# Filter time tiles of a long convolution taken in pairs: products in a tile of two PSUM banks

## The chip, the cores and the metric

The kernel runs on one core of a Trainium2 chip. The engines named below are TensorE (PE in the profile, its weight loads PEld), VectorE (DVE), ScalarE (ACT), GpSimd (POOL) and SyncE (SP), whose queue issues nearly all DMAs of this kernel. PSUM is the memory that TensorE writes; here it has eight banks of 512 fp32 columns on 128 partitions. The metric is the device time of one execution in microseconds; lower is better.

## The reference, cut to what matters

The model is two layers over 1024 latent and 256 context tokens of width 1024. Layer 0 is an attention layer, layer 1 a Hyena layer: two gated long convolutions. The filters of these convolutions aren't weights. A small network with sines makes them from position features, and an exponential decay in time is laid over them:

```python
def hyena_filter_spectra(L, w_in, w_hid, b, freq, w_out):
    ...
    for k, w in enumerate((w_in, w_hid[0], w_hid[1])):
        hdn = jnp.sin(freq[k] * (hdn @ w.astype(f32) + b[k]))
    h = (hdn @ w_out.astype(f32)).reshape(L, HY_ORDER, 2, HY_WIDTH)
    ...
    h = h * jnp.exp(-t * deltas)[:, None, None, :]
    hf, hb = h[:, :, 0], h[:, :, 1]
    k_circ = jnp.concatenate([hf[:1] + hb[:1], hf[1:], jnp.zeros_like(hf[:1]), hb[:0:-1]], axis=0)
    return jnp.fft.rfft(k_circ, axis=0)
```

There are 1024 time steps, two orders, two directions (forward and backward) and 1024 channels. The change concerns the line with the decay and the joining of the two directions.

## The kernel before, in words

**What runs beside what.** `layer0_in` opens the PSUM pool `ps0` with eight banks: three for projections (`pj`), one for the modulation vectors (`ad`), two for the filter products (tag `ph`) and two for the spectra (`pu`). It runs two generators against each other. `filters` makes the filter spectra of layer 1, which need nothing but constants. `work` makes the modulation vectors (`ada`, whose weights `adaw` are streamed through two pages) and the input projections of layer 0 (`project`: 12 matmuls of 512 columns for each step, with weights `wr` that are split into a high and a low part, L96 and L97). After each second step of `filters` comes one step of `work`. At the very start the steps of `filters` alternate with the eight steps of the first `ada`, four loads of 256 KB each.

**The filter loop.** `filter_mlp` (L181) computes the hidden activations of the network: three layers, each in two halves of 512 columns, matmul (L202), ScalarE (L203), VectorE and ScalarE again. Then 8 channel groups `g` of 128 channels follow, and in each group 8 time tiles `j` of 128 steps:

- L314 loads the decay table of the tile, 128 KB, into one of two buffers `dec`;
- four matmuls of 256 columns (L318, L319: two directions, high and low part of the weights `fw`) fill one bank, tile `ph`; two such tiles exist, so TensorE can fill one while VectorE reads the other;
- L321 multiplies the 512 columns by the decay, into `kk` (two buffers); in tile 0 a bias of one row is added (L325);
- L328 and L329 store the sum and the difference of the two directions, 256 columns each, into `kp` and `km`.

After the eight tiles, `load(g + 1)` splits the group's next weights `fwr` (an own buffer), and `ring` (L217) and `forward` (L267) take `kp` and `km` through a hand-made transform of eight blocks: some 20 VectorE operations, then for each block a split (L96, L97), 9 to 12 matmuls into `u`, a ScalarE eviction `ko` (L340) and two stores to `kd` in HBM (L351). `ring` takes two buffers of tag `rt` for three temporaries.

**What sets the order.** Each engine works off its own queue in order, and so does the SP queue: a DMA that waits for a buffer holds all that were issued behind it. The order within a queue is fixed when the program is built, from the order of the code and an estimate of when each thing is ready, so that the loads and the products of the next tiles can stand somewhat ahead of their place in the code. The attention follows when both generators are through and the pools are closed; its tiles take the space of the filter pools.

Of the kernel before, what the change touches and what calls it, by code (L numbers as in the profile page):

```python
# [11 lines left out]
F32 = mybir.dt.float32  # L12
F32R = mybir.dt.float32r
AF = mybir.ActivationFunctionType
ALU = mybir.AluOpType
# [4 lines left out]
P = 128  # L20
# [35 lines left out]
class Net:  # L56
# [124 lines left out]
    def filter_mlp(self, fp, mp, psum, ptag):  # L181
        nc, a = self.nc, self.a
        feat = mp.tile([66, L], F32, tag="rg", name="feat")
        nc.sync.dma_start(out=feat, in_=a["feat"])
        win = fp.tile([66, P], F32, name="fwin")
        whid = fp.tile([P, 2, P], F32, name="fwhid")
        nc.sync.dma_start(out=win, in_=a["fwin"])
        nc.sync.dma_start(out=whid, in_=a["fwhid"].rearrange("l p m -> p l m"))
        v, act = nc.vector, nc.scalar
        turn = fp.tile([P, 2, 3], F32, name="turn")  # L190
        v.tensor_scalar(out=turn[:, 0], in0=self.col("ff", 0, 3), scalar1=1 / (2 * math.pi), scalar2=None, op0=ALU.mult)
        v.tensor_tensor(out=turn[:, 1], in0=self.col("fb", 0, 3), in1=turn[:, 0], op=ALU.mult)
        h = feat
        magic = 12582912.0
        for l in range(3):
            w = win if l == 0 else whid[:, l - 1, :]
            arg = mp.tile([P, L], F32, tag="rg", name="arg")
            n = mp.tile([P, L], F32, tag="rg", name="nrnd")
            for s in range(2):
                sl = slice(512 * s, 512 * s + 512)  # L200
                ps = psum.tile([P, 512], F32, tag=ptag, name="pmlp")
                nc.tensor.matmul(ps, lhsT=w, rhs=h[:, sl], start=True, stop=True)  # L202
                act.activation(out=arg[:, sl], in_=ps, func=AF.Identity, scale=turn[:, 0, l : l + 1],  # L203
                               bias=turn[:, 1, l : l + 1])
                v.tensor_scalar(out=n[:, sl], in0=arg[:, sl], scalar1=magic, scalar2=-magic, op0=ALU.add, op1=ALU.add)
                v.tensor_tensor(out=arg[:, sl], in0=arg[:, sl], in1=n[:, sl], op=ALU.subtract)
                act.activation(out=n[:, sl], in_=arg[:, sl], func=AF.Sin, scale=TURN)
            h = n
        self.show("h", h)
        self.hf = fp.tile([P, L], F32R, name="hf")  # L210
        self.hr = fp.tile([P, L], F32R, name="hr")
        nc.scalar.copy(out=self.hf[0:64], in_=h[0:64])
        nc.vector.tensor_tensor(out=self.hf[64:128], in0=h[0:64], in1=self.hf[0:64], op=ALU.subtract)
        nc.scalar.copy(out=self.hr[64:128], in_=h[64:128])
        nc.vector.tensor_tensor(out=self.hr[0:64], in0=h[64:128], in1=self.hr[64:128], op=ALU.subtract)
# [68 lines left out]
    def filters(self, psum, pt_h, pt_u, side):  # L284
        nc, a = self.nc, self.a
        fp = self.open("filt", 1, side=side)
        rp = self.open("filtr", 2, side=side)
        gp = self.open("filtg", 6, side=side)
        fm = [fp.tile([P, 25, P], F32R, name=f"fm{i}") for i in range(2)]
        self.filter_mlp(fp, gp, psum, pt_h)  # L290
        last = yield
        for c in (slice(13, 19), slice(19, 25), slice(0, 7), slice(7, 13)):
            for i in range(2):
                nc.gpsimd.tensor_copy(out=fm[i][0:1, c.start, 0:1], in_=last[0:1, 0:1])
                nc.gpsimd.dma_start(out=fm[i][:, c], in_=a["fm"][i][:, c])
        two = lambda tag, dt=F32: rp.tile([P, 2, CS], dt, tag=tag, name=tag)
        ubank = lambda: psum.tile([P, 2, CS], F32, tag=pt_u, name="u")
        self.kd = self.dram.tile([2, NCH, P, 17, CS], F32, name="kd")

        def load(g):  # L300
            wr = rp.tile([P, 512], F32, tag="fwr", name="fwr", bufs=1)
            wh, wl = [rp.tile([P, 512], F32R, tag=f"fw{r}", name="fw", bufs=1) for r in range(2)]
            nc.sync.dma_start(out=wr, in_=a["fwout"][g])
            self.split(wr, wh, wl)
            return wh, wl

        nxt = load(0)
        for g in range(KD):
            wh, wl = nxt
            kp = [gp.tile([P, 4, CS], F32, tag="rg", name=f"kp{i}") for i in range(2)]  # L310
            km = [gp.tile([P, 4, CS], F32, tag="rg", name=f"km{i}") for i in range(2)]
            for j in range(8):
                dec = rp.tile([P, 2, 1, P], F32, tag="dec", name="dec", bufs=2)
                nc.sync.dma_start(out=dec, in_=a["dec"][g, j])  # L314
                ps = psum.tile([P, 2, 2, P], F32, tag=pt_h, name="ph")
                ts = slice(P * j, P * j + P)
                for d, h in ((0, self.hf), (1, self.hr)):
                    nc.tensor.matmul(ps[:, d], lhsT=h[:, ts], rhs=wh[:, 256 * d : 256 * d + 256], start=True, stop=False)  # L318
                    nc.tensor.matmul(ps[:, d], lhsT=h[:, ts], rhs=wl[:, 256 * d : 256 * d + 256], start=False, stop=True)  # L319
                kk = rp.tile([P, 2, 2, P], F32, tag="kk", name="kk")  # L320
                nc.vector.tensor_tensor(out=kk, in0=ps, in1=dec.broadcast_to([P, 2, 2, P]), op=ALU.mult)  # L321
                if j == 0:
                    bias = rp.tile([1, 2, P], F32, tag="hb", name="hbias", bufs=1)
                    nc.sync.dma_start(out=bias, in_=a["hbias"][:, :, P * g : P * g + P])
                    nc.vector.tensor_tensor(out=kk[0:1, 0], in0=kk[0:1, 0], in1=bias, op=ALU.add)  # L325
                k0 = kp[j // 4][:, j % 4].rearrange("p (o c) -> p o c", o=2)
                k1 = km[j // 4][:, j % 4].rearrange("p (o c) -> p o c", o=2)
                nc.vector.tensor_tensor(out=k0, in0=kk[:, 0], in1=kk[:, 1], op=ALU.add)  # L328
                nc.vector.tensor_tensor(out=k1, in0=kk[:, 0], in1=kk[:, 1], op=ALU.subtract)  # L329
                if j == 0:  # L330
                    nc.vector.tensor_copy(out=km[0][0:1, 0], in_=kp[0][0:1, 0])
                yield
            if g + 1 < KD:
                nxt = load(g + 1)
            cl = slice((g % 2) * P, (g % 2) * P + P)

            def emit(i, b):
                u = self.forward(two, ubank, fm, i, b)
                ko = rp.tile([P, 2, CS], F32, tag="ko", name="ko")
                nc.scalar.activation(out=ko, in_=u, func=AF.Copy, scale=1.0 / 1024)  # L340
                r0 = 2 * i + 1
                if i == 0:
                    r0 = 0
                    kx = rp.tile([P, CS], F32, tag="kx", name="kx", bufs=1)
                    nc.vector.tensor_scalar(out=ko[0:1], in0=ko[0:1], scalar1=0.5, scalar2=None, op0=ALU.mult)
                    nc.scalar.copy(out=kx, in_=ko[:, 0])
                    nc.scalar.copy(out=kx[0:1], in_=ko[0:1, 1])
                    nc.vector.memset(ko[0:1, 1], 0.0)
                for o in range(2):
                    oc = slice(P * o, P * o + P)  # L350
                    nc.sync.dma_start(out=self.kd[o, g // 2, :, r0 : r0 + 2, cl], in_=ko[:, :, oc])  # L351
                    if i == 0:
                        nc.sync.dma_start(out=self.kd[o, g // 2, :, 2, cl], in_=kx[:, oc])

            for i, b in self.ring(two, lambda: gp.tile([P, 1024], F32, tag="rg", name="rg"), kp, km, False):
                emit(i, b)
                yield
        self.close("filtg", "filtr", "filt")
# [989 lines left out]
def _features():  # L1348
    f = np.float32
    i = np.arange(L, dtype=f)  # L1350
    t = np.linspace(0.0, 1.0, L).astype(f)
    wpos = (f(2.0 * math.pi / L) * i)
    bands = np.linspace(1e-4, 15, 16).astype(f)
    ph = bands[None, :] * wpos[:, None]
    hdn = np.concatenate([t[:, None], np.cos(ph), -np.sin(ph)], axis=-1).astype(f)
    rev = (L - np.arange(L)) % L
    feat = np.concatenate([hdn.T, hdn[rev].T], axis=0)
    deltas = np.abs(np.linspace(math.log(1e-2) / 0.3, math.log(1e-2) / 1.5, D)).astype(f)
    dec = np.exp(-t[:, None] * deltas[None, :]).astype(f)
    dec = np.stack([dec, dec[rev]], axis=1)  # L1360
    dec = dec.reshape(8, P, 2, 8, P).transpose(3, 0, 1, 2, 4)
    return np.ascontiguousarray(feat), np.ascontiguousarray(dec[:, :, :, :, None, :])


def _rope():
# [9 lines left out]
def prepare(i):  # L1375
# [35 lines left out]
    a["fm"] = _dft(False)  # L1411
    a["dm"] = _dft(True)
    a["feat"], a["dec"] = _features()
    w = i["hy_filt_w_in"][0]
    o = np.zeros_like(w)
# [32 lines left out]
```

## Time and profile before

| | us |
|---|---|
| median of 3 runs | 1736.26 |
| lowest, highest | 1733.69, 1740.81 |
| profiled execution, its own time | 1731.71 |
| span of the profiled execution | 1729.9 |
| busy: TensorE, VectorE, ScalarE | 1633.5, 1442.2, 766.3 |

The filters and the input projections take the first quarter of the span, about 420 us. Shares of busy time over the whole span say little about that quarter: TensorE's 94% is mostly the attention and the convolutions behind it. So the views that count are those that can be cut to a stretch: the windows (busy time by engine in each stretch, the DMA share, bytes per second), the waits (who waited for whom), the chain of waits in order of time, and the timeline. Busy times of TensorE overstate it, because the records of neighbouring matmuls overlap; start to start, the matmuls of 512 columns stand 0.23 us apart, with durations of 0.39.

### The profile page before, as it was taken

To read this page: it belongs to the slowest core of one execution; us is meant where nothing else is said; L and a number is where in the kernel's file an instruction comes from. 1 tells how busy PE (TensorE), PEld (TensorE's weight loads), DVE (VectorE), ACT (ScalarE), POOL (GpSimd) and SP (SyncE) were. 2 spreads that over 40 slices of the span, in tenths; PEclk is the share of its full clock that TensorE was granted. 3 is DMA by queue.
4 is the path that set the end of the run, shared out by engine and by line. 5 is a ranking of instruction groups with operands and counts; after the bars stand their busy time and mean duration, and the time that the engine had idled before them with its cause. 6 is when DMAs were issued, how large, how long until landed. Compare 5 with 4: busy or idle time off the path is not lost.

```text
span 1729.9 us, 22940 instructions
## 1 busy us (share of the span) xinstructions
PE 1633.5 (94%) x8160; PEld 1299.5 (75%) x8160; DVE 1442.2 (83%) x2558; ACT 766.3 (44%) x1337; POOL 16.0 (1%) x43
## 2 busy tenths in 40 slices
PE   5899897899999999999999999999999999999996
PEld 2467676787788788788787777888888888887874
DVE  4886979895699899899899456999999999999856
ACT  4533444445455465555555345433433433343313
POOL 1000000000000000000000010000000000000000
PEclk9899999899999999999999999999999999999998
DMA  9777664436101001010014771332332332244545
GB/s 342 256 231 222 200 187 120 138 89 206 28 27 37 25 32 38 19 33 25 25 56 132 232 254 64 101 98 83 101 115 83 104 106 89 95 122 134 180 142 197
DMA packets 140759, 206.15 MB, mean 119 GB/s; under 512 B 13578, under 2 KB 71649, under 8 KB 140516
## 3 DMA queue, kind: packets, MB, share of 16 engines
q1 hardware_dynamic: 137508, 194.00, 35.7%
q0 software_dynamic: 3136, 10.69, 1.9%
q8 instruction: 64, 1.05, 0.3%
q14 instruction: 51, 0.42, 0.1%
HBM read 148.92 MB, written 53.61 MB: 117 GB/s over the span
## 4 chain that ended last, share of the span: by engine, by line
PE 75%; DVE 10%; DMA 9%; ACT 3%; issue 2%; SPq 1%; DVEq 0%; ACTq 0%
PE pj L121 12%; PE pj L119 12%; PE pj L120 12%; DMA dec<-in_dec 2%; PE O L120 2%; PE S L119 2%; PE O L119 2%; PE S L826 2%; PE O L121 2%; PE apx L762 2%; PE S L825 2%; PE S L121 2%; PE S L120 2%; PE apx L763 2%; PE fu L119 2%; PE fy L119 2%
## 5 line engine op out<-in xcount | busy, mean ns | idle before, releaser
L96 ACT CAST w<-wr 128x512 fp32r<-128x512 f32 (+1 forms) x149 | 90.7, 609 | 259.5 <-PE pj L120 129.5
L119 PE MATMUL pj<-a,w 128*128 128x512 f32 x512 | 203.1, 397 | 1.7 <-ACT a L422 1.6
L121 PE MATMUL pj<-a,w 128*128 128x512 f32 x512 | 203.1, 398 | 0.0
L120 PE MATMUL pj<-a,w 128*128 128x512 f32 x512 | 203.0, 397 | 0.0
L828 ACT ACTIVATE p<-S 128x512 f32<-128x512 f32 x160 | 95.7, 598 | 148.2 <-DVE acc L835 69.5
L97 DVE TENSOR_TENSOR w<-wr,w 128x512 fp32r<-128x512 f32 (+1 forms) x149 | 98.8, 671 | 54.7 <-ACT w L96 54.6
L96 ACT CAST bh<-raw 128x512 fp32r<-128x512 f32 x128 | 77.1, 620 | 89.1 <-DVE raw L1071 71.0
L119 PEld LDWEIGHTS pj<-a,w 128*128 128x128 f32 x512 | 96.4, 188 | 22.0 <-ACT a L422 2.4
L120 PEld LDWEIGHTS pj<-a,w 128*128 128x128 f32 x512 | 96.5, 188 | 19.9 <-DVE a L423 0.2
L121 PEld LDWEIGHTS pj<-a,w 128*128 128x128 f32 x512 | 96.6, 189 | 19.5 <-issue 0.8
L97 DVE TENSOR_TENSOR p<-p 128x512 fp32r<-128x512 f32 x160 | 109.4, 684 | 1.5 <-ACT p L96 1.2
L764 DVE TENSOR_REDUCE cm<-apx 128x1 f32<-128x512 f32 (+1 forms) x192 | 107.1, 591 | 3.8 <-PE apx L763 3.1
L835 DVE TENSOR_TENSOR acc<-acc,p 128x512 f32<-128x512 f32 x144 | 98.7, 685 | 7.6 <-ACT p L828 6.7
L121 PE MATMUL pj<-pg,w 128*128 128x512 f32 (+1 forms) x248 | 96.5, 389 | 8.7 <-DVE w L97 8.6
L96 ACT CAST p<-p 128x512 fp32r<-128x512 f32 x160 | 99.5, 622 | 4.8
L119 PE MATMUL pj<-pg,w 128*128 128x512 f32 (+1 forms) x248 | 95.7, 389 | 2.7 <-ACT pg L422 2.7
L120 PE MATMUL pj<-pg,w 128*128 128x512 f32 (+1 forms) x248 | 96.6, 389 | 0.6 <-DVE pg L423 0.6
L97 DVE TENSOR_TENSOR bl<-raw,bh 128x512 fp32r<-128x512 f32 x128 | 84.7, 686 | 9.1 <-ACT bh L96 9.0
L119 PE MATMUL u<-bh,fm 128*128 128x256 f32 (+1 forms) x200 | 68.2, 342 | 12.2 <-ACT bh L96 9.5
L762 PE MATMUL apx<-kn,qn 128*128 128x512 f32 (+1 forms) x192 | 69.0, 364 | 2.2 <-DVE cm L764 1.9
L321 DVE TENSOR_TENSOR kk<-ph,dec 128x512 f32<-128x512 f32 x64 | 42.6, 684 | 33.2 <-DMA dec<-in_dec 26.6
L763 PE MATMUL apx<-krh,r 128*128 128x512 f32 (+1 forms) x192 | 67.1, 357 | 0.0
(312 smaller groups left out, 4408.9 us busy)
## 6 DMA issues: line engine op xcount, KB each, us to landing
aw<-in_adaw SPq DMA_DIRECT2D x32, 512.0 KB
kd<-ko SPq DMA_DIRECT2D x128, 128.0 KB
wr<-in_hw SPq DMA_DIRECT2D x64, 256.0 KB
kt<-kd SPq DMA_DIRECT2D x56, 256.0 KB
wr<-in_w SPq DMA_DIRECT2D x34, 256.0 KB
dec<-in_dec SPq DMA_DIRECT2D x64, 128.0 KB
pg<-in_adaw SPq DMA_DIRECT2D x32, 256.0 KB
wr<-in_wo SPq DMA_DIRECT2D x32, 256.0 KB
```

What stands on the lines that cost most here:

```text
L96: self.nc.scalar.copy(out=hi, in_=raw)
L97: self.nc.vector.tensor_tensor(out=lo, in0=raw, in1=hi, op=ALU.subtract)
L119: mm(out, lhsT=w[0], rhs=x[0], start=start, stop=False)
L120: mm(out, lhsT=w[0], rhs=x[1], start=False, stop=False)
L121: self.last = mm(out, lhsT=w[1], rhs=x[0], start=False, stop=stop)
L321: nc.vector.tensor_tensor(out=kk, in0=ps, in1=dec.broadcast_to([P, 2, 2, P]), op=ALU.mult)
L762: mm(b[:, :w], lhsT=qn[0][:, c], rhs=kn[0][:, o : o + w], start=True, stop=False)
L763: mm(b[:, :w], lhsT=r1[:, c], rhs=krh[:, o : o + w], start=False, stop=True)
L764: v.tensor_reduce(out=cm[:, t, i : i + 1], in_=b[:, :w], axis=AX.X, op=ALU.max)
L825: mm(S, lhsT=krh[:, c], rhs=r1, start=False, stop=False)
L828: act.activation(out=p, in_=S, func=AF.Exp, scale=ASCALE)
L835: v.tensor_tensor(out=acc, in0=acc, in1=p, op=ALU.add)
```

## The change

Two time tiles are taken together. The products of a pair go into one PSUM tile of two banks, of which there is one (`bufs=1`). One decay product covers 1024 columns, sum and difference cover 512 each, one decay load brings 256 KB; `dec` still has two buffers, now of a pair each, and `kk` has one of a pair. The pair yields twice at its end, so the count of steps stays. The network's small matmuls (L202) use the same PSUM tag and so have one tile instead of two. The raw weights `wr` in `load` take a buffer of tag `rt` instead of their own. The decay tables are laid out anew on the host.

```diff
-                ps = psum.tile([P, 512], F32, tag=ptag, name="pmlp")
+                ps = psum.tile([P, 2, 512], F32, tag=ptag, name="pmlp", bufs=1)[:, s]
...
-            wr = rp.tile([P, 512], F32, tag="fwr", name="fwr", bufs=1)
+            wr = two("rt").rearrange("p a c -> p (a c)")
...
-            for j in range(8):
-                dec = rp.tile([P, 2, 1, P], F32, tag="dec", name="dec", bufs=2)
-                nc.sync.dma_start(out=dec, in_=a["dec"][g, j])
-                ps = psum.tile([P, 2, 2, P], F32, tag=pt_h, name="ph")
-                ts = slice(P * j, P * j + P)
-                for d, h in ((0, self.hf), (1, self.hr)):
-                    nc.tensor.matmul(ps[:, d], lhsT=h[:, ts], rhs=wh[:, 256 * d : 256 * d + 256], start=True, stop=False)
-                    nc.tensor.matmul(ps[:, d], lhsT=h[:, ts], rhs=wl[:, 256 * d : 256 * d + 256], start=False, stop=True)
-                kk = rp.tile([P, 2, 2, P], F32, tag="kk", name="kk")
-                nc.vector.tensor_tensor(out=kk, in0=ps, in1=dec.broadcast_to([P, 2, 2, P]), op=ALU.mult)
+            for j in range(0, 8, 2):
+                dec = rp.tile([P, 2, 2, 1, P], F32, tag="dec", name="dec", bufs=2)
+                nc.sync.dma_start(out=dec, in_=a["dec"][g, j // 2])
+                ps = psum.tile([P, 2, 2, 2, P], F32, tag=pt_h, name="ph", bufs=1)
+                for i in range(2):
+                    ts = slice(P * (j + i), P * (j + i) + P)
+                    for d, h in ((0, self.hf), (1, self.hr)):
+                        w = slice(256 * d, 256 * d + 256)
+                        nc.tensor.matmul(ps[:, i, d], lhsT=h[:, ts], rhs=wh[:, w], start=True, stop=False)
+                        nc.tensor.matmul(ps[:, i, d], lhsT=h[:, ts], rhs=wl[:, w], start=False, stop=True)
+                kk = rp.tile([P, 2, 2, 2, P], F32, tag="kk", name="kk", bufs=1)
+                flat = lambda t, o: t.rearrange("p i d o c -> p (i d) o c")
+                nc.vector.tensor_tensor(out=flat(kk, 2), in0=flat(ps, 2), in1=flat(dec, 1).broadcast_to([P, 4, 2, P]),
+                                        op=ALU.mult)
...
-                k0 = kp[j // 4][:, j % 4].rearrange("p (o c) -> p o c", o=2)
-                k1 = km[j // 4][:, j % 4].rearrange("p (o c) -> p o c", o=2)
-                nc.vector.tensor_tensor(out=k0, in0=kk[:, 0], in1=kk[:, 1], op=ALU.add)
-                nc.vector.tensor_tensor(out=k1, in0=kk[:, 0], in1=kk[:, 1], op=ALU.subtract)
+                for out, op in ((kp, ALU.add), (km, ALU.subtract)):
+                    k = out[j // 4][:, j % 4 : j % 4 + 2].rearrange("p i (o c) -> p i o c", o=2)
+                    nc.vector.tensor_tensor(out=k, in0=kk[:, :, 0], in1=kk[:, :, 1], op=op)
                 if j == 0:
                     nc.vector.tensor_copy(out=km[0][0:1, 0], in_=kp[0][0:1, 0])
+                yield
                 yield
...
-    dec = dec.reshape(8, P, 2, 8, P).transpose(3, 0, 1, 2, 4)
-    return np.ascontiguousarray(feat), np.ascontiguousarray(dec[:, :, :, :, None, :])
+    dec = dec.reshape(4, 2, P, 2, 8, P).transpose(4, 0, 2, 1, 3, 5)
+    return np.ascontiguousarray(feat), np.ascontiguousarray(dec[:, :, :, :, :, None, :])
```

More of the change, by code (lines that the diff above doesn't have):

```diff
@@ L324, in filters @@
                     nc.sync.dma_start(out=bias, in_=a["hbias"][:, :, P * g : P * g + P])
-                    nc.vector.tensor_tensor(out=kk[0:1, 0], in0=kk[0:1, 0], in1=bias, op=ALU.add)
-                k0 = kp[j // 4][:, j % 4].rearrange("p (o c) -> p o c", o=2)
-                k1 = km[j // 4][:, j % 4].rearrange("p (o c) -> p o c", o=2)
-                nc.vector.tensor_tensor(out=k0, in0=kk[:, 0], in1=kk[:, 1], op=ALU.add)
-                nc.vector.tensor_tensor(out=k1, in0=kk[:, 0], in1=kk[:, 1], op=ALU.subtract)
+                    nc.vector.tensor_tensor(out=kk[0:1, 0, 0], in0=kk[0:1, 0, 0], in1=bias, op=ALU.add)
+                for out, op in ((kp, ALU.add), (km, ALU.subtract)):
+                    k = out[j // 4][:, j % 4 : j % 4 + 2].rearrange("p i (o c) -> p i o c", o=2)
+                    nc.vector.tensor_tensor(out=k, in0=kk[:, :, 0], in1=kk[:, :, 1], op=op)
                 if j == 0:
                     nc.vector.tensor_copy(out=km[0][0:1, 0], in_=kp[0][0:1, 0])
+                yield
                 yield
```

## The prediction

> **What bounds the kernel now.** I read the page first, then only the stretch that the change touches, by windows, waits, the chain of waits and the timeline.
>
> ```profile
> span 1729.9 us, 22940 instructions
> L321 DVE TENSOR_TENSOR kk<-ph,dec 128x512 f32<-128x512 f32 x64 | 42.6, 684 | 33.2 <-DMA dec<-in_dec 26.6 <-PE ph L319 6.6
> ...
> 23.00:50.00 27.00, 16.34 (x90) 6.97 (x88) 16.10 (x37) 3.92 (x6) 0.00 (x0) 0.84 1.08 387
> 118.00:169.00 51.00, 48.22 (x266) 36.43 (x265) 34.02 (x71) 17.29 (x31) 0.00 (x0) 1.00 0.81 246
> 213.00:257.00 44.00, 43.24 (x235) 34.76 (x234) 34.62 (x75) 18.89 (x32) 0.00 (x0) 1.00 0.65 198
> 257.00:300.00 43.00, 33.26 (x201) 28.18 (x200) 39.56 (x83) 19.91 (x39) 0.00 (x0) 0.92 0.39 117
> 342.00:379.00 37.00, 36.83 (x199) 31.66 (x200) 33.84 (x70) 15.37 (x28) 0.00 (x0) 1.00 0.39 111
> ```
>
> The page's row of the decay product says two things: 64 instructions cost VectorE 42.6 us, and VectorE stood idle 33.2 us in front of them, 26.6 of it for the decay table. The window rows (from:to, length, then busy time of PE, PEld, DVE, ACT, POOL, the granted clock, the DMA share, GB/s) show that the bound changes. From 23 to 50 us the DMA engines are full (share 1.08). From 213 to 257 and from 342 to 379 TensorE is full (43.24 of 44, 36.83 of 37). From 257 to 300 it is VectorE (39.56 of 43). So one kind of saving can't count everywhere.
>
> ```profile
> DVE kk L321 <- DMA dec<-in_dec: 26.6, 16, 5.2
> DVE kk L321 <- PE ph L319: 6.6, 5, 2.1
> ...
> PE ph L318 <- DVE kk L321: 1.9, 3, 1.0
> ...
> SPq L314 <- DVE rms L405: 7.9, 1, 7.9
> ...
> 27.66 0.33 SPq L314 DMA_DIRECT2D dec<-in_dec  x1
> ```
>
> These are rows of the waits (total, times, longest) from 23 to 400 us; the fourth is the SP queue's own from 19 to 30, and the last a row of SP's timeline. The decay table is waited for 16 times. TensorE hardly waits for a free product tile: 1.9 us. The SP queue stood 7.9 us behind one decay load, from about 20 us until a decay buffer came free at 27.66; behind it stood `adaw` loads.
>
> ```profile
> 43.92 4.81 DMA dec<-in_dec
> ...
> 152.44 5.33 DMA dec<-in_dec
> ...
> 201.29 3.67 DMA wr<-in_w
> ...
> 246.10 3.50 DMA dec<-in_dec
> 249.72 0.70 DVE kk L321
> 250.44 3.78 DMA dec<-in_dec
> ...
> 372.42 3.29 DMA dec<-in_dec
> ```
>
> In the chain of waits (start, length, what) a decay load is the link again and again. A load leaves when its buffer is free, lands 3.3 to 5.3 us later, and the product behind it frees the buffer for the next. 249.72 to 250.44 is the pattern in full: load, product, load.
>
> **The change part by part.** *VectorE.* A pair in the fourth group, where nothing is waited for:
>
> ```profile
> 254.32 1.29 DVE L321 TENSOR_TENSOR kk<-ph,dec 128x512 f32<-128x512 f32 x2 [0.47 <-DMA dec<-in_dec]
> 255.53 0.42 DVE L328 TENSOR_TENSOR kp<-kk 128x256 f32<-128x256 f32 x1
> 255.86 0.42 DVE L329 TENSOR_TENSOR km<-kk 128x256 f32<-128x256 f32 x1
> 256.19 0.42 DVE L328 TENSOR_TENSOR kp<-kk 128x256 f32<-128x256 f32 x1
> 256.53 0.42 DVE L329 TENSOR_TENSOR km<-kk 128x256 f32<-128x256 f32 x1
> 256.87 2.36 DVE L225 TENSOR_TENSOR rg<-kp,kp 128x1024 f32<-128x1024 f32 x2
> ...
> L225 DVE TENSOR_TENSOR rg<-kp,kp x16: 1218/1219/1223, 50.2 to 379.5; 128x1024 f32<-128x1024 f32 x16
> ```
>
> The pair takes 256.87 - 254.32 = 2.55 us. Instructions that don't depend on each other start 0.33 us apart at 256 columns and 0.60 apart at 512 (1.29 less one duration of 0.684), less than their durations: 0.07 us is the fixed part, 0.53 or 0.27 the columns. Afterwards the product of 1024 columns costs 1.22 (the L225 row has that shape), the sum must wait for its end, and sum and difference take 0.60 each: 2.45 us. That saves 0.10 on each of 32 pairs, 3.2 us. Where the two tiles of a pair stood apart today, each product was waited out: 0.69 (such a product stands in the row of 33.14 below) and 2 x 0.33, twice, 2.7 a pair, which saves 0.27, or 8.6 us if all were so. About half are, from groups that mostly wait for DMA; I take 5 us of VectorE's time, and 3 of it on the path, since VectorE is the bound in about six tenths of the stage.
>
> [...] By the rows the 96 instructions at 0.07 us are 6.4 us, and the dependence takes half of it away.
>
> *Decay loads.* 64 loads become 32 of twice the size. Two buffers now hold four tiles, so at the start of a group two pairs are there instead of two tiles, and the third pair's load leaves when the first product is through, a whole pair before it is needed. A load of 256 KB took 3.67 (`wr`, above), no longer than the loads of 128 KB beside it; the full DMA engines at 387 GB/s would add 128 KB / 387 = 0.34 us. A pair costs VectorE 2.45 us plus a weight split, TensorE some 3.7 us (next row), so the load is due about when it lands. What goes is bounded by 26.6 us and by zero. By place:
>
> ```profile
> 157.87 1.29 DVE L321 TENSOR_TENSOR kk<-ph,dec 128x512 f32<-128x512 f32 x2 [5.09 <-DMA dec<-in_dec]
> ...
> 249.72 1.29 DVE L321 TENSOR_TENSOR kk<-ph,dec 128x512 f32<-128x512 f32 x2 [5.25 <-DMA dec<-in_dec]
> ...
> 242.12 0.39 PE L119 MATMUL pj<-pg,w 128*128 128x512 f32 x1
> ...
> 244.87 0.28 PE L318 MATMUL ph<-fw,hf 128*128 128x256 f32 x1
> 244.98 0.28 PE L319 MATMUL ph<-fw,hf 128*128 128x256 f32 x1
> ...
> 250.50 0.36 PE L318 MATMUL ph<-fw,hf 128*128 128x256 f32 x1
> ...
> 158.81 0.28 PE L318 MATMUL ph<-fw,hf 128*128 128x256 f32 x1
> ...
> 33.14 0.69 DVE L321 TENSOR_TENSOR kk<-ph,dec 128x512 f32<-128x512 f32 x1 [1.63 <-DMA dec<-in_dec]
> ...
> 48.83 0.69 DVE L321 TENSOR_TENSOR kk<-ph,dec 128x512 f32<-128x512 f32 x1 [1.66 <-DMA dec<-in_dec]
> ```
>
> At 249.72 the products of the last pair come from TensorE only at 250.50 plus eight matmuls at 0.115 us each (244.98 - 244.87), so its decay product can't start before 251.6; with 2.45 and 0.2 for the signal, `ring` starts at 254.3, not 256.87: 2.5 us of the 5.25 are gained. At 157.87 TensorE reaches the third pair at 158.81 whatever the table does, since it stands behind a modulation step; with 0.9 for the matmuls, 2.45, one projection step (244.87 - 242.12 = 2.75) and the last pair, I get 2.5 us of the 5.09. The other waits after 50 us sum to 26.6 - 5.1 - 5.3 - 9.9 = 6.3, of which I take a half, 3 (9.9 is the sum of six waits from 33.14 to 48.83, the first and the last of them above). Those 9.9 stand under full DMA engines and would stay; but the SP queue is released from its 7.9 us, and later decay loads no longer stand behind two `adaw` steps each. The bytes don't change. I take 2 us, between 0 and 5. Sum: 2.5 + 2.5 + 3 + 2 = 10 us.
>
> *What it costs.* The pair's product waits for eight matmuls, not four: 4 x 0.115 = 0.46 us wherever VectorE waits for TensorE; 5 times today, 2.3 us at most, I take 1. With one product tile, the next pair's matmuls wait for the whole product of the last pair. Behind them in TensorE's queue stands a projection step of 2.75 us. In between TensorE has that step to do, while VectorE needs about 1.4 (signal and product): covered, unless VectorE is late. Today's wait is 1.9 us; I take 2 more, with 0 and 14 as ends (24 pairs after 118 us, 0.6 us each, the time by which the end of a double product lies behind that of a first single one). The other rows that the sum, the rivals and the tests need (the network's evictions, the split of the raw weights, ScalarE's wait for the stores, the start of the last `ring`):
>
> ```profile
> L203 ACT ACTIVATE arg<-pmlp,turn x6: 769/779/780, 7.5 to 19.1; 128x512 f32<-128x512 f32 x6
> ...
> 252.56 0.68 DVE L97 TENSOR_TENSOR fw<-fwr,fw 128x512 fp32r<-128x512 f32 x1
> ...
> ACT ko L340 <- DMA kd<-ko: 17.3, 11, 5.7
> ...
> 378.38 2.35 DVE L225 TENSOR_TENSOR rg<-kp,kp 128x1024 f32<-128x1024 f32 x2
> ```
>
> In the network the second half now waits for the eviction of the first: three layers lose about 0.78 + 0.2 each, 3 us, at 5 to 23 us. The full DMA engines hide it; without that cover it would be 3. The raw weights in `rt`: a temporary of `ring` waits for their split, which stands ahead of `ring` on VectorE anyway; nothing, at most one split of 0.68 in some groups. SP issues 32 loads fewer; no engine waits on that, but the queue moves up. The steps of `work` keep their places.
>
> Sum: -3 - 10 + 1 + 2 = -10 us. Against the profiled execution's own 1731.71 that is 1721.7; the median of the runs lies 4.55 above that execution, so the forecast is **1726 us**.
>
> **The rivals.** *All waits go.* If the freed waits after 50 us are gained whole (16.7) with 5 at the start and 5 of VectorE, less 3, it is -24: 1712. Against it: TensorE's full stretches. *Something else is next.* The waits turn into others: TensorE is full in 81 us of the stage, `ko` waits 17.3 us for its stores, the modulation loads are late. Then nothing or 3 us is gained: 1735. For it speaks that a decay load can be a link of the chain while the next link is ready just behind. *One product tile is too few.* TensorE's queue is in order; where VectorE is late with a pair's product, TensorE stops at the next pair's matmuls, and the projection step behind them, which was ready, stands too. It decides where TensorE reaches the next pair less than 1.4 us after the last matmul of the one before, as when the order at build time puts two pairs close together. Price: 24 x 0.6 = 14 us, with the gain of VectorE lost to it: 1736 + 12 = 1748. Against it: today two tiles cost 1.9 us only, and a projection step lies between pairs.
>
> [...] No row before shows the kernel with one tile.
>
> **How the numbers follow.** Forecast 1726 (1718 to 1732): 0.48. All waits go, 1712: 0.14. Something else is next, 1735: 0.23. One tile is too few, 1748: 0.15. The range reaches from the first rival to halfway between the other two: 1711 to 1742. A measurement of this kernel can tell about 0.5%, 8.7 us, from no change: below 1727.6 is faster, above 1744.9 slower. The forecast lies close to that bound; I give three quarters of it to faster, with the first rival 0.50; the rest of it and the second rival make 0.35 the same; 0.15 slower.
>
> **What would show it.** In the profile after: the product of 1024 columns at 1.22 us, sums at 0.68; its wait for the decay table well below 26.6 us, and 5 us or less after 50 us; the last `ring` starting some 10 us ahead of today's 378.4; TensorE's wait for the decay product near 4 us. If that wait is above 10 us, the last rival holds. If the decay wait is gone and the last `ring` isn't earlier, the second does. If the decay wait stays, my reading of the prefetch is wrong.

## The result, and the profile after

| | before | after |
|---|---|---|
| median, us | 1736.26 (7 runs) | 1728.07 (7 runs) |
| lowest, highest | 1733.69, 1740.81 | 1724.16, 1732.69 |
| ratio, 95% interval | | 0.9949 [0.9933, 0.9966] |
| profiled execution | 1731.71 | 1728.13 |

The kernel became 8.2 us faster; 10 were forecast (1726). The interval leaves out 1, but it lies around the bound of 0.5% that the prediction named: the median of 1728.07 misses its 1727.6 by 0.5 us and so counts as the same, to which it gave 0.35, where faster had 0.50. The profiled execution of before lies below the lowest time of its row, that of after on its median, so the two traces differ by 3.6 us only. A trace shows where the waits went; the size of an effect is taken from the medians.

The page's first line, and the groups by line from 23 to 400 us (busy us, mean ns | idle time before them, and what ended it):

```profile
span 1726.3 us, 22764 instructions
```

```profile
L324 DVE TENSOR_TENSOR kk<-ph,dec 128x1024 f32<-128x1024 f32 x32 | 39.0, 1220 | 23.6 <-PE ph L321 22.0 <-DMA dec<-in_dec 1.2
L332 DVE TENSOR_TENSOR kp<-kk 128x512 f32<-128x512 f32 x32 | 22.0, 687 | 0.5
L332 DVE TENSOR_TENSOR km<-kk 128x512 f32<-128x512 f32 x32 | 21.8, 682 | 0.0
```

The wait for the decay table fell from 26.6 us to 1.2. But VectorE now stands 22.0 us in front of the same product for TensorE, where it stood 6.6. The waits of after, and below them the row of before that the prediction didn't show (total, times, longest):

```profile
DVE kk L324 <- PE ph L321: 22.0, 11, 5.7
DVE w L97 <- ACT w L96: 19.7, 8, 5.7
PE ph L320 <- DVE kk L324: 5.2, 5, 1.4
DVE kk L324 <- DMA dec<-in_dec: 1.2, 1, 1.2
```

```profile
DVE w L97 <- ACT w L96: 12.8, 4, 7.7
```

The windows from 23 to 400 us, before and then after (busy time of PE, PEld, DVE, ACT, POOL, clock, DMA share, GB/s):

```profile
23.00:400.00 377.00, 330.03 (x1792) 249.44 (x1791) 308.44 (x649) 162.31 (x293) 0.00 (x0) 0.94 0.61 191
```

```profile
23.00:400.00 377.00, 323.55 (x1794) 247.97 (x1794) 304.88 (x549) 163.18 (x295) 2.71 (x6) 0.95 0.62 192
```

VectorE was idle 377 - 308.44 = 68.6 us before and is idle 72.1 us after. Counted only up to the last transform, which comes sooner after the change, the idle time is 355.38 - 287.83 = 67.6 and 350.48 - 284.09 = 66.4. The 25 us of waits for the table are not gone as idle time: other releasers took their place. VectorE's timeline shows it at the two places that the prediction worked out:

```profile
158.93 1.22 DVE L324 TENSOR_TENSOR kk<-ph,dec 128x1024 f32<-128x1024 f32 x1 [3.17 <-PE ph L321]
...
162.61 1.23 DVE L324 TENSOR_TENSOR kk<-ph,dec 128x1024 f32<-128x1024 f32 x1 [0.65 <-PE ph L321]
...
165.55 1.22 DVE L225 TENSOR_TENSOR rg<-kp,kp 128x1024 f32<-128x1024 f32 x1
...
244.36 1.23 DVE L324 TENSOR_TENSOR kk<-ph,dec 128x1024 f32<-128x1024 f32 x1 [3.76 <-PE ph L321]
...
252.88 0.39 DVE L171 TENSOR_TENSOR adac<-ad,cols 128x8 f32<-128x8 f32 x4 [2.22 <-PE ad L165]
253.83 1.22 DVE L324 TENSOR_TENSOR kk<-ph,dec 128x1024 f32<-128x1024 f32 x1 [0.56 <-PE ph L321]
...
256.77 2.36 DVE L225 TENSOR_TENSOR rg<-kp,kp 128x1024 f32<-128x1024 f32 x2
```

The table isn't waited for any more, but TensorE is. The transform (L225) at 256.77 starts where it did (256.87). The other one, at 165.55, started in the trace of before at

```profile
169.28 2.36 DVE L225 TENSOR_TENSOR rg<-kp,kp 128x1024 f32<-128x1024 f32 x2
```

so there 3.7 us are gained, and at 256.77 nothing. The last sum of after, and the transform behind it:

```profile
372.27 0.69 DVE L332 TENSOR_TENSOR kp<-kk 128x512 f32<-128x512 f32 x1
...
373.48 2.35 DVE L225 TENSOR_TENSOR rg<-kp,kp 128x1024 f32<-128x1024 f32 x2
```

The last transform starts at 373.48, 4.9 us ahead of 378.38. The attention's first matmul, before and after:

```profile
439.78 0.73 PE L762 MATMUL apx<-kn,qn 128*128 128x512 f32 x2
```

```profile
438.19 0.73 PE L766 MATMUL apx<-kn,qn 128*128 128x512 f32 x2
```

1.6 us are left of the 4.9 there. Between the filters' end and the attention TensorE still has projections of layer 0 to do, which don't depend on the filters.

These places are those of one execution each, and they move from one to the next. In the second trace of the same changed kernel (after_again, below), the last transform starts at

```profile
377.66 2.35 DVE L225 TENSOR_TENSOR rg<-kp,kp 128x1024 f32<-128x1024 f32 x2
```

and the other two at 169.80 and 260.70. So the 3.7 and the 4.9 us were not seen twice. Over eight traces of this case (before, the change twice, mlp_pu twice, loads_only, half_products and no_diff) the attention's start (432.8 to 447.1 us) and the time of the execution (1721.6 to 1740.4) go together; what comes behind that start takes 1285.1 to 1291.5 us of the span, though its code is the same.

### The profile page after: what moved, and what is told of

Its sections match the earlier page's. It is cut to its first block, busy times and chain, and to the rows that moved or that the text cites. A ratio compares the mean times of both kernels' runs of the same rounds, so it can differ in the third digit from the quotient of the medians.

```text
span 1726.3 us, 22764 instructions
## 1 busy us (share of the span) xinstructions
PE 1625.8 (94%) x8160; PEld 1295.0 (75%) x8160; DVE 1437.6 (83%) x2462; ACT 768.6 (45%) x1341; POOL 15.2 (1%) x43
## 4 chain that ended last, share of the span: by engine, by line
PE 78%; DMA 8%; DVE 7%; ACT 2%; issue 1%; SPq 1%; DVEq 0%; ACTq 0%
PE pj L121 13%; PE pj L119 13%; PE pj L120 13%; DMA aw<-in_adaw 3%; PE apx L766 2%; PE apx L767 2%; PE S L119 2%; PE O L120 2%; PE S L830 2%; PE O L119 2%; PE O L121 2%; PE S L829 2%; PE S L120 2%; PE S L121 2%; PE fu L119 2%; PE fy L119 2%
## 5 line engine op out<-in xcount | busy, mean ns | idle before, releaser
L119 PE MATMUL u<-bh,fm 128*128 128x256 f32 (+1 forms) x200 | 67.5, 339 | 18.7 <-ACT bh L96 11.6
L119 PE MATMUL fy<-bh,dm 128*128 128x256 f32 (+1 forms) x200 | 64.1, 321 | 2.4 <-ACT bh L96 2.4
```

The source lines that it names most:

```text
L119: mm(out, lhsT=w[0], rhs=x[0], start=start, stop=False)
```

## The experiments

All ratios are to the kernel before on the same chip: its median was 1737.65 in the first group of four, 1737.81 in the second, of three, and 1736.80 in the third, of four.

| run | us | ratio, 95% interval |
|---|---|---|
| loads_only | 1728.12 | 0.9952 [0.9936, 0.9967] |
| one_dec | 1734.76 | 0.9986 [0.9968, 1.0005] |
| two_tiles | 1727.84 | 0.9952 [0.9934, 0.9970] |
| mlp_pu | 1725.52 | 0.9937 [0.9917, 0.9957] |
| sums_only | 1734.82 | 0.9982 [0.9963, 1.0002] |
| small_loads | 1734.30 | 0.9977 [0.9961, 0.9993] |
| no_loads | 1728.21 | 0.9949 [0.9929, 0.9969] |
| after_again (the change) | 1730.30 | 0.9959 [0.9943, 0.9974] |
| pu_again (mlp_pu) | 1726.03 | 0.9940 [0.9923, 0.9956] |
| half_products | 1721.81 | 0.9906 [0.9882, 0.9930] |
| no_diff | 1735.76 | 0.9995 [0.9980, 1.0010] |

The theory was the prediction's: the gain comes from loads that leave earlier. The rivals were that fewer VectorE instructions carry it, or that the single product tile gives a part of it back. A third rival is the clock granted to TensorE, which differs between the runs. In the twelve runs of sums_only, the fastest, 1728.87 us, had 0.980 of full speed and the slowest, 1740.50, 0.971. Averaged over the runs it was 0.977 for the kernel before in all three groups, 0.978 for loads_only, 0.981 and 0.980 for the change, and 0.981 for mlp_pu and for pu_again. So the gain of the loads alone stands at nearly the clock of before, and the clock isn't its cause. Differences of 2 or 3 us between runs whose clocks differ by 0.003 can't be put down to the waits alone, and no run tells whether the clock sets the time or the other way round.

### The loads alone

The kernel before, with only the loads changed; the raw weights in tag `rt` make the room.

```diff
-                dec = rp.tile([P, 2, 1, P], F32, tag="dec", name="dec", bufs=2)
-                nc.sync.dma_start(out=dec, in_=a["dec"][g, j])
+                if j % 2 == 0:
+                    pair = rp.tile([P, 2, 2, 1, P], F32, tag="dec", name="dec", bufs=2)
+                    nc.sync.dma_start(out=pair, in_=a["dec"][g, j // 2])
+                dec = pair[:, j % 2]
```

> The kernel before with the decay tables of 256 KB in two buffers (and the raw weights in the tag rt) alone; products, sums and product tiles stay per time tile. If the gain of the change is the earlier loads, this has all of it: the wait for the decay table falls from 26.6 us to about 1, ratio to before 0.993 to 0.996, some 1726 us. If the gain is fewer and longer VectorE instructions, the wait falls as well but the time stays: ratio 0.998 to 1.001.

0.9952: as much as the whole change, with the 64 products, the 128 sums and differences and the two product tiles of before. It also keeps the network's two tiles, which the change gives up; run mlp_pu, below, has them too. The raw weights' move to `rt` comes with the larger buffers here, and no run has it alone. Its row of the groups by line:

```profile
L323 DVE TENSOR_TENSOR kk<-ph,dec 128x512 f32<-128x512 f32 x64 | 42.0, 683 | 26.6 <-PE ph L321 17.4 <-DMA dec<-in_dec 8.9
```

The wait for the table fell to 8.9, not to about 1. The waits cut at 50 us tell why, first those of the loads alone, then those of the change (the row from 23 to 50 us, then those from 50 to 400):

```profile
DVE kk L323 <- DMA dec<-in_dec: 8.9, 2, 4.9
...
DVE kk L323 <- PE ph L321: 16.8, 11, 6.0
```

```profile
DVE kk L324 <- PE ph L321: 5.7, 1, 5.7
...
DVE kk L324 <- PE ph L321: 16.4, 10, 3.8
DVE kk L324 <- DMA dec<-in_dec: 1.2, 1, 1.2
```

Before 50 us the loads alone still wait 8.9 us for the table, where 9.9 stood: the prediction said that these would stay. In the change VectorE waits there 5.7 us for the first products instead, and the table has landed meanwhile; so this part of its fall to 1.2 is no gain of the loads. From 50 us on the table's wait falls from 16.7 to nothing and to 1.2, and the wait for TensorE is the same in both, 16.8 and 16.4. The products keep their width in the one and not in the other, so the new wait isn't made by the wider product.

### One pair of the table ahead

The changed kernel with one decay buffer.

```diff
-                dec = rp.tile([P, 2, 2, 1, P], F32, tag="dec", name="dec", bufs=2)
+                dec = rp.tile([P, 2, 2, 1, P], F32, tag="dec", name="dec", bufs=1)
```

> The changed kernel with one decay buffer of a pair in place of two: each load can leave only when the last product is through. If the earlier loads are the gain, the wait for the decay table comes back, 30 to 60 us of VectorE idle, and the time is that of before or worse: ratio 1.000 to 1.015. If fewer VectorE instructions are the gain, the ratio stays near 0.996.

```profile
L324 DVE TENSOR_TENSOR kk<-ph,dec 128x1024 f32<-128x1024 f32 x32 | 39.1, 1221 | 33.2 <-PE ph L321 16.1 <-DMA dec<-in_dec 14.5 <-PE ad L128 2.5
```

The wait for the table came back to 14.5 us, less than the 30 to 60 expected, and most of the gain went: 1737.65 x (0.9986 - 0.9952) = 5.9 of 8.3 us against the loads alone; the ratio stayed below the 1.000 to 1.015 that were expected. The same wide instructions without a table ahead leave 0.14%, with an interval that takes in no gain. The wait needn't be long to cost: 13.9 of the 14.5 us lie behind 50 us, where 16.7 stood before, so there nearly all of the wait came back. The trace is of one of its slowest executions (1741.94).

### Two product tiles

The changed kernel with two tiles of one bank, two products of 512 columns into the pair's `kk`, and the network's two tiles back; loads and sums of a pair stay.

```diff
-                ps = psum.tile([P, 2, 2, 2, P], F32, tag=pt_h, name="ph", bufs=1)
                 for i in range(2):
+                    ps = psum.tile([P, 2, 2, P], F32, tag=pt_h, name="ph")
...
+                    nc.vector.tensor_tensor(out=kk[:, i], in0=ps, in1=dec[:, i].broadcast_to([P, 2, 2, P]), op=ALU.mult)
```

> The changed kernel with two product tiles of one bank again, two decay products of 512 into the pair's kk, and the network's matmuls on two tiles; loads and sums stay paired. If the single product tile takes back a part of the gain (VectorE waits 22.0 us for the products after the change, 6.6 before), this is 2 to 5 us faster than the change: ratio to before 0.991 to 0.994, and that wait falls below 12. If the wait for the products is only what the decay loads hid (TensorE is simply not there yet), the time stays at 0.995 and the wait stays near 20.

0.9952, the same as the change. From the waits of this run, and from its groups by line:

```profile
PE ph L321 <- DVE kk L323: 3.2, 5, 1.6
```

```profile
L323 DVE TENSOR_TENSOR kk<-ph,dec 128x512 f32<-128x512 f32 x64 | 42.0, 680 | 22.7 <-DMA dec<-in_dec 11.6 <-PE ph L322 10.6 <-DVE rms L405 0.4
```

TensorE waits 3.2 us for a free product tile instead of 5.2, and VectorE's wait for the products fell to 10.6, below the 12 that was named; the table's is 11.6 again, and the time didn't move. The run gives the network its two tiles back as well, so the run to compare it with is the next, mlp_pu, in which the network has two tiles too, though those of the spectra: 1725.52 with one product tile against 1727.84 with two. A single tile for the filter products costs nothing that these runs can tell.

### The network on two tiles

The changed kernel, but the network's small matmuls use the spectra's two PSUM tiles, which stand empty then.

```diff
-                ps = psum.tile([P, 2, 512], F32, tag=ptag, name="pmlp", bufs=1)[:, s]
+                ps = psum.tile([P, 512], F32, tag=ptag, name="pmlp")
...
-        self.filter_mlp(fp, gp, psum, pt_h)
+        self.filter_mlp(fp, gp, psum, pt_u)
```

> The changed kernel with the network's matmuls on the two tiles of the spectra, so that they are double again. The first product comes near 27 us as before the change, not 35. If the late first product costs nothing because the loads of the first 57 us are what counts, the time stays that of the change, 0.995. If it costs, 1 to 4 us come: 0.992 to 0.994.

1725.52, the lowest of the group of four. Its interval overlaps with the change's; the second pair of runs puts both on one chip:

> The changed kernel itself, to stand beside the three kernels below on one chip. Ratio 0.993 to 0.997, as first measured (0.9949).

> The changed kernel with the network's small matmuls on the spectra's two PSUM tiles, once more, beside the change itself. If the network's lost double buffer costs the change something (the first products ten microseconds later), it lies 1.5 to 3 us below the change, ratio near 0.9935; if the later start is made up for by 50 us, both give the same within 1 us.

On one chip: 1730.30 (1726.14 to 1731.31, 7 runs) for the change, 1726.03 (1724.38 to 1729.13, 6 runs) for this one, 4.3 us less by the medians and 3.3 by the ratios to before (0.9959 and 0.9940); the two intervals still overlap. Twice it was the faster, which makes a gain likely and doesn't show its size. The timelines of TensorE and VectorE at the start, the change first:

```profile
27.36 1.93 PE L128 MATMUL ad<-pg,sc 128*32 128x512 f32 x8 [5.03 <-DMA pg<-in_adaw]
33.21 1.94 PE L128 MATMUL ad<-pg,sc 128*32 128x512 f32 x8 [3.92 <-DMA pg<-in_adaw]
35.07 0.58 PE L320 MATMUL ph<-fw,hf 128*128 128x256 f32 x1
```

```profile
28.74 1.22 DVE L213 TENSOR_TENSOR hf<-nrnd,hf 64x1024 fp32r<-64x1024 f32 x1 [0.25 <-ACT hf L212]
...
36.88 1.22 DVE L324 TENSOR_TENSOR kk<-ph,dec 128x1024 f32<-128x1024 f32 x1 [5.67 <-PE ph L321]
...
51.40 1.22 DVE L225 TENSOR_TENSOR rg<-kp,kp 128x1024 f32<-128x1024 f32 x1
```

and of the second run with the network on two tiles:

```profile
24.61 0.58 PE L320 MATMUL ph<-fw,hf 128*128 128x256 f32 x1 [1.72 <-DVE hf L213]
...
27.44 1.94 PE L128 MATMUL ad<-pg,sc 128*32 128x512 f32 x8
```

```profile
23.34 1.22 DVE L213 TENSOR_TENSOR hf<-nrnd,hf 64x1024 fp32r<-64x1024 f32 x1
...
27.55 1.22 DVE L324 TENSOR_TENSOR kk<-ph,dec 128x1024 f32<-128x1024 f32 x1 [0.26 <-PE ph L321]
...
48.64 2.35 DVE L225 TENSOR_TENSOR rg<-kp,kp 128x1024 f32<-128x1024 f32 x2
```

With one tile the hidden activations `hf` are 5.4 us later (28.74 against 23.34). In TensorE's queue two modulation steps then stand ahead of the first products, and these wait for `adaw` pages; so the first product is made at 35.07, not at 24.61. By the first transform most of it is made up for: 51.40 against 48.64. With the network on two tiles VectorE waits 8.6 us for the table between 23 and 50 us, and with one tile the loads land while the products are late.

### Fewer VectorE instructions alone, and depth without size

The kernel before with a pair's `kk`, sums and differences of 512 columns, everything else as it was:

```diff
+                kk = rp.tile([P, 2, 2, 2, P], F32, tag="kk", name="kk", bufs=1)
...
+                    nc.vector.tensor_tensor(out=kk[:, i], in0=ps, in1=dec.broadcast_to([P, 2, 2, P]), op=ALU.mult)
...
+                for out, op in ((kp, ALU.add), (km, ALU.subtract)):
+                    k = out[j // 4][:, j % 4 : j % 4 + 2].rearrange("p i (o c) -> p i o c", o=2)
+                    nc.vector.tensor_tensor(out=k, in0=kk[:, :, 0], in1=kk[:, :, 1], op=op)
```

> The kernel before with only the sums and differences of a pair taken together (512 columns, 64 instructions fewer); loads of 128 KB in two buffers and two product tiles as before. Theory (the earlier table loads are the gain): VectorE's instructions are worth nothing, ratio 0.998 to 1.003, wait for the table still above 20 us. Rival (fewer VectorE instructions carry a part of the gain, as the prediction had it with 3 of 10 us): ratio 0.995 to 0.998. If the sums of a pair hold back its second product's buffer, it is slower by up to 0.3%.

and the kernel before with four decay buffers of 128 KB:

```diff
-                dec = rp.tile([P, 2, 1, P], F32, tag="dec", name="dec", bufs=2)
+                dec = rp.tile([P, 2, 1, P], F32, tag="dec", name="dec", bufs=4)
```

> The kernel before with four decay buffers of 128 KB in place of two (the raw weights in tag rt make the room, as in the change); 64 loads as before. If what counts is how far ahead the loads may run (256 KB more of table on the chip), it gains what the change gains: ratio 0.993 to 0.997, wait for the table near 9 us. If the size or the count of the loads counts (32 instead of 64 of them, each with its own time to land), it gains less than half: ratio 0.998 to 1.001, wait above 15 us.

The groups by line of both, the sums first:

```profile
L323 DVE TENSOR_TENSOR kk<-ph,dec 128x512 f32<-128x512 f32 x64 | 42.3, 682 | 36.1 <-DMA dec<-in_dec 25.2 <-PE ph L322 10.9
```

```profile
L321 DVE TENSOR_TENSOR kk<-ph,dec 128x512 f32<-128x512 f32 x64 | 42.3, 682 | 30.6 <-PE ph L319 20.7 <-DMA dec<-in_dec 9.6
```

The sums alone give 0.9982 with an interval that takes in 1.0002: between nothing and 6 us, on the border of the two expectations, and the wait for the table stays. The small loads fall between the two theories. Their waits are those of the loads alone (9.6 and 20.7 against 8.9 and 17.4), so the depth takes the wait away as the larger loads do; but the time is 0.9977, half the gain. So the length of this wait alone doesn't set the time. Whether the other half lies in the 32 more loads isn't settled: the intervals [0.9961, 0.9993] and [0.9936, 0.9967] overlap.

### What bounds the filters afterwards

Three runs take work from one resource each. The first uses the tables of the first two pairs for all pairs, which leaves out 30 of the 32 loads:

```diff
-                dec = rp.tile([P, 2, 2, 1, P], F32, tag="dec", name="dec", bufs=2)
-                nc.sync.dma_start(out=dec, in_=a["dec"][g, j // 2])
+                if g == 0 and j < 4:
+                    tabs.append(rp.tile([P, 2, 2, 1, P], F32, name=f"dec{j}", bufs=1))
+                    nc.sync.dma_start(out=tabs[-1], in_=a["dec"][g, j // 2])
+                dec = tabs[(j // 2) % 2]
```

> The changed kernel with the decay tables of the first two pairs used for all pairs: 30 of 32 decay loads (7.5 MB) are left out, so no wait for a table is left behind the first group, and the DMA engines have that much less to move. If the table were still what holds the filters, and time won there reached the end, it takes 10 to 20 us off the changed kernel: ratio to the kernel before 0.983 to 0.990. If the waits only move to TensorE's products and to the weight splits, as VectorE's unchanged idle time in the change suggests, it stays within 5 us of the change: ratio 0.992 to 0.996, with VectorE's wait for TensorE's product above 20 us.

The second leaves out the low part of the products (`rhs=wl`), the third the differences (the transform takes the sums twice, and `km` isn't allocated):

```diff
-                        nc.tensor.matmul(ps[:, i, d], lhsT=h[:, ts], rhs=wl[:, w], start=False, stop=True)
```

> The changed kernel without the low-part product of the filters: 128 matmuls of 256 columns at 0.115 us, 14.7 us of TensorE's time, are left out; VectorE's work and the loads stay. If TensorE's work and its fixed gaps bound the stage after the change, 10 to 15 us come off the changed kernel (ratio to the kernel before 0.986 to 0.989). If VectorE bounds it, under 4 us come off (0.993 to 0.996), though its waits for the products shrink.

```diff
-                for out, op in ((kp, ALU.add), (km, ALU.subtract)):
+                for out, op in ((kp, ALU.add),):
```

> The changed kernel without the differences of the two directions (the transform takes the sums twice): 32 instructions of 512 columns and 8 copies of one row are left out, 32 x 0.60 = 19.2 us of VectorE's time. If VectorE bounds the stage after the change, 10 to 19 us come off the changed kernel (ratio 0.984 to 0.989). If TensorE does, under 4 us come off (0.993 to 0.996). If they take turns, both this and the run without low-part products give about half.

Without the loads: 0.9949, the change's own ratio. So the loads have no more to give that the interval would show; the change, and the loads alone, have taken it. Without 14.7 us of TensorE's work: 0.9906 against the change's 0.9959 beside it, 8.5 us by the medians, more than half. That lies between the 10 to 15 expected if TensorE bounds the filters and the 4 if VectorE does. Without 19.2 us of VectorE's: 0.9995, 5.5 us slower than the change, which none of the expectations had. The row of the groups by line of the first, and the rows of the waits of the second and third:

```profile
L327 DVE TENSOR_TENSOR kk<-ph,dec 128x1024 f32<-128x1024 f32 x32 | 39.0, 1219 | 15.4 <-PE ph L324 14.8
```

```profile
DVE kk L323 <- PE ph L320: 7.6, 5, 3.8
```

```profile
DVE kk L323 <- PE ph L320: 44.3, 17, 11.4
```

Where TensorE has less to do, VectorE waits 7.6 us for it; where VectorE has less to do, it waits 44.3. (Without the loads it is 14.8, less than the 20 expected.) So after the change TensorE's work is on the path, and nothing shows that VectorE's is. That the order of TensorE's queue matters beside its work is argued, not shown. Why the run without differences is slower than the change, not equal to it, stays open; TensorE had the same work. In its records the products of some pairs stand later in TensorE's order, and one of them is waited for 11.4 us, but no run tells whether that is the cause.

Some of TensorE's idle time belongs to no change here. Its longest stop before the attention is the first matmul of a transform, in before and in after:

```profile
308.64 1.46 PE L119 MATMUL u<-bh,fm 128*128 128x512 f32 x2 [7.46 <-ACT bh L96]
```

```profile
307.89 0.80 PE L119 MATMUL u<-bh,fm 128*128 128x512 f32 x1 [8.85 <-ACT bh L96]
```

```profile
299.02 2.35 DVE L225 TENSOR_TENSOR rg<-kp,kp 128x1024 f32<-128x1024 f32 x2
```

VectorE works on that transform from 299.02 on, and TensorE stands at that matmul until its first block is split: 8.85 us, not less than the 7.46 of before.

## Why the prediction was right, and where it wasn't

The forecast of 1726 came within 2.1 us of the median of 1728.07, and the two main mechanisms held: the loads carry the gain, and the removed waits are not gained whole. Some of its terms were wrong, in both directions.

- **Decay loads, -10.** Right, and somewhat too large: the loads alone measured 1737.65 - 1728.12 = 9.5 us by medians, 8.3 by the ratio, and leaving the loads out altogether adds nothing. By place it was mixed. At 157.87 the prediction had 2.5 us; the transform there starts 3.7 us earlier. At 249.72 it had 2.5 as well; there the transform came at 256.77 and nothing was gained, because the second pair's product had become the wait (244.36, 3.76 us for TensorE), and VectorE then waited 2.22 us for a modulation step ahead of the last pair (252.88). The second trace of the change shows neither gain (169.80 and 260.70), so by place the terms are not settled. The bound from TensorE's next products was right in kind: it is what ends the wait. (Its sum there counts the 0.2 us of the signal twice: 251.6 + 2.45 is 254.05, not 254.3. The trace of before has such a step: the last matmul of a product starts at 241.53, and VectorE's product at 241.85, which is 0.115 and 0.2 us later.)
- **At the start, -2.** This part of the decay loads was not seen in the change: the first transform starts 1.2 us later than the 50.2 of before. With the network on two tiles it starts at 48.64, 1.6 us earlier. So the start gains about what was said while the network keeps two tiles, and the lost tile takes it back.
- **VectorE's instructions, -3.** Open. The sums alone give 3 us with zero in their interval, and 19.2 us less for VectorE afterwards win nothing. The loads alone reach the change's time without any of it, but they keep the network's two tiles; against mlp_pu, which keeps them too, they are 2.6 us slower (1728.12 and 1725.52), with overlapping intervals and a granted clock of 0.978 against 0.981. The durations were right (product 1.22, sums 0.69 and 0.68, 0.61 apart), though the 96 instructions less (32 products, 64 sums and differences) at 0.07 us make 6.7 us, not 6.4. What wasn't shown is the share on the path, six tenths: the prediction has no row for it, and after the change VectorE waits for products 16.4 us behind 50 us.
- **The product from PSUM, 1.22.** Right: it takes 1220 ns on average at 1024 columns; the operations of the same shape from SBUF took 1219 at the median in the prediction's row of L225.
- **The product waits for eight matmuls, +1.** The wait for TensorE rose from 6.6 to 22.0 us, but not by this: with single products and loads of a pair it is 17.4 already, and behind 50 us 16.8 against the change's 16.4. The lone effect wasn't tried by itself.
- **One product tile, +2.** TensorE's wait for VectorE is 5.2 us, near the 4 that was named as the test. Of the two runs with the network on two tiles, the one with a single product tile isn't the slower (1725.52 and 1727.84). The cost is not measurable; the rival with 14 us (1748) fell.
- **The network's lost tile, 0 ("The full DMA engines hide it").** This step failed. The cover holds only in part: the network lost 5.4 us instead of 3, the modulation steps went ahead of the first products, and 2.8 us were left at the first transform. At the end two tiles for the network are 4.3 us better than the change beside it by the medians, 3.3 by the ratios, with overlapping intervals.
- **Two buffers.** For the decay tables the second buffer carries most of the gain: the change with one stands at 0.9986, with two at 0.9949. For the product tile, which isn't filled by a DMA, a second one shows no gain in these runs (1727.84 us with two, 1725.52 with one, the network on two tiles in both).
- **Something else is next (1735).** The rival was right in its mechanism and wrong in its size. The waits did become others (22.0 for products, 19.7 for weight splits), and the last transform came 4.9 us earlier in one trace and 0.7 in the other, not the 10 that the prediction gave as its sign. But 8.2 of the 10 us arrived in the medians.

So the total was in part met by luck. The network's cost was set to nothing, where the runs beside each other differ by 3.3 us, and 3 us were charged for the eight matmuls and the single product tile, which no run shows as a cost; these errors happen to cancel. That the loads carry the gain is shown by the times: theirs alone, and their loss with one buffer. By which waits it reaches the end of the kernel isn't shown, since four small buffers end the same wait for half the gain. What remains open as well is the rest between traces and medians. The profiles differ by 3.6 us, the medians by 8.2. The runs of before reach from 1727 to 1745 us over the three groups, those of the change from 1724 to 1733; one profile can't show why.

The version with the lowest time of those that compute the same is the change with the network on the spectra's tiles: 0.9937 and 0.9940 in two measurements.

## What to carry to other kernels

A prefetch that was one buffer short showed up here as many waits of a few microseconds for the load (16, the longest 5.2 us, 26.6 in all); try the loads first, larger and further ahead, since they alone were worth as much as the whole change here (0.9952 and 0.9949); depth with small loads was worth half (0.9977). Then expect the wait to move to the next late engine, as it did here (for TensorE 6.6 us before, 22.0 after): read how soon that engine's data would have come, and count only the difference. Where a run joins several edits, compare it with one that differs in a single edit, and take sizes from several executions. When a tile is shared, look at every user of its tag, also at the one-off code at the start, and ask what the builder will put into the gap that a slower start leaves.

## What the runs showed of the hardware

A load of twice the size landed hardly later here, 3.4 us after its issue for 256 KB and 3.1 for 128 KB, both at the median. The DMA issues of the run with four small buffers and of the change (count, KB each, median us to landing):

```profile
dec<-in_dec SPq DMA_DIRECT2D x64, 128.0 KB, 3.1
```

```profile
dec<-in_dec SPq DMA_DIRECT2D x32, 256.0 KB, 3.4
```

The prediction's estimate for the double size was 0.34 us more; these rows are 0.3 apart. The agreement is loose: in the first trace of the change the loads of 256 KB land 3.0 to 4.6 us after their issue.
